# A two-layer retention/gMLP trunk on one core: gatings started one job later, loads split and moved, another square root at the end

## The chip, the core and the metric

The kernel runs on one NeuronCore of a Trainium2 chip. The metric is the device time of one execution in microseconds (us), smaller is better. Matrix products run on TensorE (PE, with its weight loads as PEld), elementwise work on VectorE (DVE) and ScalarE (ACT), and SyncE (SP) issues nearly all DMAs, in the order in which they are written. In the traces each engine takes its instructions in the order of the program, so an instruction that waits holds up all that is queued behind it on its engine.

## The reference, cut to what matters

288 tokens (256 of a prompt, 32 of a sample), model width 2048, two layers. Each layer normalises its input, multiplies it by one wide input matrix and feeds two branches; the branches are projected, gated, merged, projected again and added to the input. A final RMSNorm follows. Everything is float32.

```python
def mixer_layer(x, s0, pos, ret_chunk, norm_g, w_in, ws, ws_b, ln_g, ln_b,
                w_ret_out, w_mlp_out, w_o):
    h = rmsnorm(x, norm_g)
    z = h @ w_in
    q, k, v, gr, u, vm, gm, ar, am = jnp.split(z, _split_points(), axis=-1)
    ...
    r_branch = (jax.nn.silu(gr) * o) @ w_ret_out
    u = jax.nn.gelu(u, approximate=False)
    vn = layernorm(jax.nn.gelu(vm, approximate=False), ln_g, ln_b)
    m = spatial_gate(u, vn, ws, ws_b)
    m_branch = (jax.nn.silu(gm) * m) @ w_mlp_out
    merged = jax.nn.sigmoid(ar) * r_branch + jax.nn.sigmoid(am) * m_branch
    return x + merged @ w_o, s_new, vn
```

`spatial_gate` multiplies, in each of 8 channel groups, the layer-normed `vm` by a 128x128 position matrix `ws`, adds a bias, and multiplies by `u`. The final step is `y = x * rsqrt(mean(x^2) + eps) * final_g`.

## The kernel before

Activations lie with channels on partitions and the 288 tokens along the free dimension. A float32 product is made from three products of float32r operands: a weight tile `raw` is cast by ACT to `whi` (`to_hi`, L105), DVE subtracts to get the rest `wlo` (`to_lo`, L108), and `mm3` (L111 to L113) issues whi times the high part of the activations (`Ah`/`Bh`), whi times the low part (`Al`/`Bl`), and wlo times the high part.

The work is a list of **jobs** (L617 on): one job multiplies 256 output channels by all 2048 input channels and hands the sum in PSUM (`ps`) to an `evac_...` function. A job has four **pieces** of 4 contraction tiles each: one weight load of 512 KB, one cast, one subtraction and 24 matmuls. The main loop (from L767) writes out, for each piece, the cast of the piece four ahead, the subtraction three ahead and the load seven ahead, then the 24 matmuls, and then a `tick`: every active generator runs to its next `yield`. The evac functions and the gatings are such generators, so what they issue falls between the pieces, on each engine behind what was written before.

In each layer eight VM jobs come first. `evac_vm` transposes them through DRAM (`zd`) into a token-major tile `vmacc`, applies GELU, and the last one forms the layer norm's statistics (`state["ln"]`). Then come the jobs U0, GM0, U1, GM1 ... U7, GM7, then AM and MLP, Q/K/V/GR, AR, RET and the output projection.

A **gating** (`sgu_gen`, L281) belongs to a group g. It needs five small loads (`load_sgu`, L267: `c0`, `c1`, `wh`, `wsr`, `wsq`), zeroes a corner of the position matrix (memset, L292), scales the normed `vm` (L299, L301), splits it into `vh` (ACT) and `vl` (DVE), issues ten matmuls on TensorE (L324 to L326), and adds bias and multiplies by u (L328 to L332). It is started ahead of U job g (L631). Gating 0 issues its own loads when it starts and then waits, tick by tick, for the statistics; each gating issues the loads of the next one after its `vh`. So gating 1 starts eight pieces after gating 0, whether gating 0 is through or not.

```python
        for g in range(NPR):
            job(U0 + g, hs, evac_u, g, lambda l, g: start(sgu_gen(l, g)))
            job(GM0 + g, hs, evac_gm, g)
```

At the **start** (L711 on) SP loads the norm's gain `ng`, the first 256 channels of x (`vmacc<-in_x`), half of piece 0's weights, the next 256 channels, the other half, and then piece 1's weights, x and further pieces in turn. TensorE meanwhile runs 10 products of a zero tile (`WARM`, L717). ACT makes six zero copies (L734, L736) that are needed in the retention part alone.

At the **end** `evac_last` (L606) takes the last job in two halves, `rs_gen(last)` (L163) sums the squares over channels on TensorE, and DVE takes 1/sqrt by a bit trick and three Newton steps (`newton`, L86, 11 small instructions and a wide one that spreads the result over 128 columns, L98). TensorE turns it to the channel layout by three products with the identity (L188 to L190), and DVE scales the output (L822, L825) as it is stored.

Of the kernel before, what the change touches and what calls it, by code (L numbers as in the profile page):

```python
# [9 lines left out]
F32 = mybir.dt.float32  # L10
# [3 lines left out]
ALU = mybir.AluOpType  # L14
# [22 lines left out]
LOOK = 3  # L37
WARM = 10
RAW = 4
# [3 lines left out]
def trunk(ctx: ExitStack, tc: tile.TileContext, a, o):  # L43
# [18 lines left out]
    ident = st([P, P], "ident")  # L62
    ones = st([P, 4], "ones")
    cos = st([P, T], "cos")
    sin = st([P, T], "sin")
# [3 lines left out]
    fg = st([P, NK], "fg")  # L69
    zero = st([P, P], "wsr", bufs=2)  # L70
    qdh = [st([P, P], f"qdh{i}", F32R) for i in range(2)]
# [91 lines left out]
    def rs_gen(last=None):  # L163
# [18 lines left out]
        v = st([P, 3], "rsv")  # L182
        V.tensor_scalar(out=v, in0=p[:, 0:3], scalar1=1.0 / DM, scalar2=EPS, op0=ALU.mult, op1=ALU.add)
        yb = newton(v, 3, "rs", st([P, 3, P], "z", bufs=3))
        yield
# [4 lines left out]
        PE.matmul(p[:, 256:288], yb[:, 2], ident[:, 96:128], start=True, stop=True)  # L190
        if last is not None:
            state["rs"] = p[:, 0:T]
        else:
            rs = st([P, T], "rsb")
            S.copy(out=rs, in_=p[:, 0:T])
            S.copy(out=rst, in_=yb[:, :, 0])
            yield
            state["rs"] = rs
            cr, sr = st([P, T], "cosr"), st([P, T], "sinr")
            V.tensor_tensor(out=cr, in0=cos, in1=rs, op=ALU.mult)  # L200
            V.tensor_tensor(out=sr, in0=sin, in1=rs, op=ALU.mult)
            state["cr"], state["sr"] = cr, sr

# [77 lines left out]
    def sgu_gen(l, g):  # L281
        if g == 0:
            load_sgu(l, 0)
        lg, lb, bs, wr, wq = state.pop(("sgu", g))
# [47 lines left out]
        V.tensor_tensor(out=sg, in0=sg, in1=state.pop(("u", g)), op=ALU.mult)  # L332
        state["s", g] = sg

    def evac_u(l, g, ps):
# [236 lines left out]
    def evac_o(l, c, ps):  # L572
        x = state.pop(("x", c))
        V.tensor_tensor(out=x, in0=ps[:, :, 0:T], in1=x, op=ALU.add)
        if l + 1 < DEPTH:
            hs = state["h"]
            prep_hi(hs, c, x, ng[:, l + 1])
            sq = add_sq(c, x)
            next(sq)
            yield  # L580
            prep_lo(hs, c, x, ng[:, l + 1])
            run(sq)
            load(xs[:, 2 * c:2 * c + 2], x)
            if c == NPR - 1:
                state.pop("rs")
                start(rs_gen())
        else:
            if c == 0:
                state["yg"] = st([P, NPR, 2, T], "vmacc")
            scale_out(c, x, 0)  # L590
            scale_out(c, x, 1)
            sq = add_sq(c, x)
            next(sq)
            yield
            run(sq)
# [24 lines left out]
    for l in range(DEPTH):  # L620
# [7 lines left out]
        for c in range(NPR):  # L628
            job(VM0 + c, hs, evac_vm, c)
        for g in range(NPR):  # L630
            job(U0 + g, hs, evac_u, g, lambda l, g: start(sgu_gen(l, g)))  # L631
            job(GM0 + g, hs, evac_gm, g)
        job(AM0, hs, evac_am, 0)
# [22 lines left out]
    def emit_raw(s):  # L656
# [4 lines left out]
        r = st([P, KP, 256], "raw", bufs=RAW)  # L661
        n = KP if s else KP // 2
        for k in range(0, KP, n):
            yield
            load(r[:, k:k + n], wsrc(l, pair)[:, i * KP + k:i * KP + k + n])
        raws[s] = r
# [23 lines left out]
    def start(gen):  # L690
        active.append(gen)
# [15 lines left out]
    def prep0(c):  # L707
        prep_hi(hs0, c, x0[:, c], ng[:, 0])
        prep_lo(hs0, c, x0[:, c], ng[:, 0])

    V.memset(zero, 0.0)  # L711
    V.memset(ones, 0.0)
# [4 lines left out]
    for _ in range(WARM):  # L717
        PE.matmul(warm[:, 0:P], zero, zero, start=True, stop=True)
    load(ng, a["norm_g"])
    load0(0)  # L720
    first = emit_raw(0)
    next(first)
    next(first)
    load0(1)
    run(first)
    run(emit_raw(1))
    load0(2)
    load0(3)
    run(emit_raw(2))
    load0(4)  # L730
    load0(5)
    run(emit_raw(3))
    for q in qdh + qdl:
        S.copy(out=q, in_=zero)  # L734
    for q in w2s:
        S.copy(out=q, in_=zero)  # L736
    prep0(0)
    h0 = st([P, KP, 256], "whi", F32R, bufs=LOOK + 2)
    l0 = st([P, KP, 256], "wlo", F32R, bufs=LOOK + 1)
    r0 = raws.pop(0)  # L740
    for k in range(0, KP, KP // 2):
        ks = slice(k, k + KP // 2)
        if k:
            prep0(1)
        to_hi(r0[:, ks], h0[:, ks])
        to_lo(r0[:, ks], h0[:, ks], l0[:, ks])
    halves[0] = h0, l0
# [7 lines left out]
    prep0(5)  # L755
    run(emit_raw(4))
    load0(6)
    load0(7)
    run(emit_raw(5))
    for n, t in (("ident", ident), ("cos", cos), ("sin", sin), ("kdec", kdec), ("qdec", qdec),  # L760
                 ("final_g", fg)):
        load(t, a[n])
    emit_hi(3)
    run(emit_raw(6))

# [3 lines left out]
    for s, (j, i) in enumerate(pieces):  # L769
        l, pair, ops, fn, c, pre = jobs[j]  # L770
        emit_hi(s + LOOK + 1)
        emit_lo(s + LOOK)
        run(emit_raw(s + LOOK + RAW))
        if s == 1:
# [17 lines left out]
        def mm(k, jj):  # L792
# [4 lines left out]
                start=(kt == 0), stop=(kt == NK - 1))  # L797

        if j == last and i == NPC - 1:
            for jj in range(2):  # L800
                for k in range(KP):
                    mm(k, jj)
                last_sq = evac_last(jj, c, po[jj][:, 0:T])
        else:
            for k in range(KP):
# [8 lines left out]
        if s == 5:  # L814
            start(rs_gen())

    while active:
# [99 lines left out]
```

## Time and profile before

| | |
|---|---|
| time, median of 3 runs | 2361.43 us (2360.75 to 2362.48) |
| the profiled execution: its time / its span | 2362.0 us / 2360.2 us |
| PE busy | 2335.9 us (99% of the span) |
| PEld busy | 2333.9 us (99%) |
| DVE busy / ACT busy | 1424.1 us (60%) / 1020.2 us (43%) |
| mean DMA rate | 189 GB/s |
| granted TensorE clock, mean over the span | 0.995 of full |

The span runs from the first to the last instruction of one profiled execution; 1.8 us of that execution's time lie around it. "Busy" of PE counts overlapping, pipelined matmuls, so 99% says that it is seldom without work, and not that it runs at its peak. A row of the waits names the engine and line that waited, what it waited for, the total, the times and the longest. In a timeline, a row has start, duration, engine, line and operation, `out<-in`, and in brackets the idle time of that engine just before and what ended it.

### The profile page before, as it was taken

How to read it: one execution, taken by the hardware profiler on the slowest of the kernel's cores; microseconds unless marked ns; L12 is line 12 of the kernel's file. 1: busy time of each engine (PE TensorE's matmuls, PEld its weight loads, DVE VectorE, ACT ScalarE, POOL GpSimd, SP SyncE). 2: the span in 40 equal slices, each digit the busy share in tenths (PEclk: the TensorE clock that was granted, in tenths of full speed). 3: DMA queues.
4: the chain of work that ended last, by engine and by line, in shares of the span. 5: the costliest groups of instructions: out<-in, count | busy, mean ns of one | idle time of the engine just before them, and what ended most of it. 6: DMA issues, size and time to landing. Idle time of an engine off the chain costs nothing.

```text
span 2360.2 us, 42693 instructions
## 1 busy us (share of the span) xinstructions
PE 2335.9 (99%) x17572; PEld 2333.9 (99%) x17572; DVE 1424.1 (60%) x2145; ACT 1020.2 (43%) x1298; POOL 0.2 (0%) x4
## 2 busy tenths in 40 slices
PE   9999999999999999999999999999999999999997
PEld 9999999999999999999999999999999999999997
DVE  7567764446777774455555777544467777645554
ACT  6445543333444453334444445433344444433342
POOL 0000000000000000000000000000000000000000
PEclk9999999999999999999999999999999999999999
DMA  8855554556778785456688555445577877744553
GB/s 268 234 171 180 175 173 163 168 165 185 219 206 230 201 223 173 163 168 193 210 218 229 165 176 177 163 163 168 172 203 198 222 206 212 219 164 162 169 196 115
DMA packets 350164, 446.36 MB, mean 189 GB/s; under 512 B 193552, under 2 KB 254736, under 8 KB 349968
## 3 DMA queue, kind: packets, MB, share of 16 engines
q1 hardware_dynamic: 349968, 443.63, 62.1%
q8 instruction: 138, 2.26, 0.4%
q14 instruction: 58, 0.48, 0.1%
HBM read 412.09 MB, written 31.46 MB: 188 GB/s over the span
## 4 chain that ended last, share of the span: by engine, by line
PE 96%; DVE 2%; issue 1%; DMA 1%; SPq 0%; ACT 0%; DVEq 0%; ACTq 0%
PE ps L111 31%; PE ps L112 31%; PE ps L113 31%; PE aux L112 1%; PE aux L113 1%; PE aux L111 1%; DMA raw<-in_w_in 1%; PE aux L324 0%; DVE wlo L108 0%; DMA vmacc<-zd 0%; SPq L78 0%; PE aux L325 0%; DVE vmacc L825 0%; DVE vmacc L299 0%; PE aux L423 0%
## 5 line engine op out<-in xcount | busy, mean ns | idle before, releaser
L108 DVE TENSOR_TENSOR wlo<-raw,whi 128x1024 fp32r<-128x1024 f32 (+1 forms) x705 | 858.0, 1218 | 509.3 <-PE ps L113 321.5
L105 ACT CAST whi<-raw 128x1024 fp32r<-128x1024 f32 (+1 forms) x705 | 733.2, 1047 | 817.8 <-PE ps L112 659.1
L111 PE MATMUL ps<-Ah,whi 128*128 128x288 f32 x2816 | 832.6, 296 | 1.4 <-ACT whi L105 1.4
L113 PE MATMUL ps<-Ah,wlo 128*128 128x288 f32 x2816 | 832.0, 295 | 0.7 <-DVE wlo L108 0.7
L112 PE MATMUL ps<-Al,whi 128*128 128x288 f32 x2816 | 831.2, 295 | 0.0
L111 PE MATMUL ps<-Bh,whi 128*128 128x288 f32 x2784 | 825.2, 296 | 0.0
L112 PE MATMUL ps<-Bl,whi 128*128 128x288 f32 x2784 | 823.8, 296 | 0.0
L113 PE MATMUL ps<-Bh,wlo 128*128 128x288 f32 x2784 | 823.8, 296 | 0.0
L111 PEld LDWEIGHTS ps<-Ah,whi 128*128 128x128 f32 x2816 | 529.8, 188 | 1.9 <-ACT whi L105 1.9
L113 PEld LDWEIGHTS ps<-Ah,wlo 128*128 128x128 f32 x2816 | 529.3, 188 | 1.4 <-DVE wlo L108 1.4
L112 PEld LDWEIGHTS ps<-Al,whi 128*128 128x128 f32 x2816 | 529.1, 188 | 0.0
L112 PEld LDWEIGHTS ps<-Bl,whi 128*128 128x128 f32 x2784 | 524.4, 188 | 0.0
L111 PEld LDWEIGHTS ps<-Bh,whi 128*128 128x128 f32 x2784 | 523.9, 188 | 0.0
L113 PEld LDWEIGHTS ps<-Bh,wlo 128*128 128x128 f32 x2784 | 523.4, 188 | 0.0
L209 DVE TENSOR_TENSOR z<-ps,rsb 128x576 f32<-128x576 f32 x52 | 39.3, 755 | 61.7 <-PE ps L113 61.7
L512 ACT ACTIVATE on<-aux,gnb,gny 128x256 f32<-128x256 f32 x48 | 23.6, 562 | 65.4 <-DVE gnb L508 65.4
L216 DVE STREAM_TRANSPOSE zt<-ps 128x512 f32<-128x512 f32 x32 | 22.9, 715 | 39.8 <-PE ps L113 38.2
L503 DVE BATCH_NORM_STATS2 gst<-aux 128x6 f32<-128x256 f32 x48 | 17.5, 421 | 34.5 <-PE aux L113 34.5
L355 ACT ACTIVATE z<-z 128x576 f32<-128x576 f32 x16 | 11.0, 687 | 46.3 <-DVE z L209 46.3
L384 DVE TENSOR_TENSOR zu<-ps,cosr 128x576 f32<-128x576 f32 x16 | 12.1, 758 | 30.6 <-PE ps L113 30.6
L375 DVE TENSOR_TENSOR vmacc<-ps,z 128x576 f32<-128x576 f32 x16 | 12.1, 758 | 30.6 <-PE ps L113 30.6
L328 DVE TENSOR_TENSOR rqh<-aux,wh 128x256 f32<-128x256 f32 x32 | 13.4, 419 | 27.8 <-PE aux L325 27.8
(221 smaller groups left out, 1146.1 us busy)
## 6 DMA issues: line engine op xcount, KB each, us to landing
raw<-in_w_in SPq DMA_DIRECT2D x511, 512.0 KB, 4.7
raw<-in_w_mlp SPq DMA_DIRECT2D x64, 512.0 KB, 4.6
raw<-in_w_ret SPq DMA_DIRECT2D x64, 512.0 KB, 4.6
raw<-in_w_o SPq DMA_DIRECT2D x64, 512.0 KB, 4.6
zd<-zt SPq DMA_DIRECT2D x224, 96.0 KB, 3.7
vmacc<-zd SPq DMA_DIRECT2D x56, 384.0 KB, 5.8
c<-in_dmask SPq DMA_DIRECT2D x16, 208.0 KB, 4.8
vmacc<-in_x SPq DMA_DIRECT2D x8, 288.0 KB, 6.8
```

What stands on the lines that cost most here:

```text
L105: S.copy(out=hi, in_=src)
L108: V.tensor_tensor(out=lo, in0=src, in1=hi.bitcast(F32), op=ALU.subtract)
L111: PE.matmul(out, lh, rh, start=start, stop=False)
L112: PE.matmul(out, lh, rl, start=False, stop=False)
L113: PE.matmul(out, ll, rh, start=False, stop=stop)
L209: V.tensor_tensor(out=z, in0=ps[:, :, 0:T], in1=bc2(state["rs"]), op=ALU.mult)
L216: V.transpose(out=zt[:, :, 0:8], in_=src[:, :, 0:TP].rearrange("p j (b t) -> p j b t", t=TS))
L328: V.tensor_tensor(out=x, in0=p[:, :, 1], in1=bs[:, 0:TP].rearrange("p (b i) -> p b i", b=2), op=ALU.add)
L375: V.tensor_tensor(out=state["acc"][:, c], in0=ps[:, :, 0:T], in1=state.pop(("sig", c)), op=ALU.mult)
L384: V.tensor_tensor(out=r, in0=ps[:, :, 0:T], in1=bc2(cr), op=ALU.mult)
L503: V.bn_stats(out=bst[:, b], in_=src[b])
L512: S.activation(out=on[:, b], in_=src[b], func=AF.Identity, bias=nb[:, b:b + 1], scale=y[:, b:b + 1])
```

## The change

1. **Order of the gatings.** The jobs run U0, U1, GM0, U2, GM1 ... U7, GM6, GM7, and gating g starts ahead of U(g+1) (the last ahead of GM7). The five loads of gating 0 are issued ahead of VM job 5.
2. **The start.** `ng` and the first contraction tile of piece 0's weights are issued by ACT. SP issues x in halves first, then the second tile, the other two, then the next x and piece 1. Cast and subtraction go tile by tile, and piece 0's matmuls go by term (two of whi times high, two of whi times low, two of wlo times high per tile). The warm-up has 5 products instead of 10. The six zero copies move to after piece 24.
3. **The end.** The 1/sqrt is ACT's Sqrt, DVE's reciprocal and one Newton step. A diagonal matrix is made from it in three DVE instructions, each followed by a product with a tile of ones. That tile and a first use of Sqrt (which brings the table load) are placed at the first job of the last projection.

```diff
-WARM = 10
+WARM = 5
...
     def rs_gen(last=None):
...
+        if last is not None:
+            y, t = st([P, 3], "rsy", bufs=2), st([P, 3], "rst", bufs=2)
+            S.activation(out=t, in_=v, func=AF.Sqrt)
+            V.reciprocal(out=y, in_=t)
+            V.scalar_tensor_tensor(out=t, in0=y, scalar=-0.5, in1=y, op0=ALU.mult, op1=ALU.mult)
+            V.tensor_tensor(out=t, in0=t, in1=v, op=ALU.mult)
+            V.scalar_tensor_tensor(out=y, in0=t, scalar=1.5, in1=y, op0=ALU.add, op1=ALU.mult)
+            dg = st([P, 3, P], "z", bufs=3)
+            p = aux()
+            for b, n in ((0, P), (1, P), (2, TS)):
+                V.tensor_scalar(out=dg[:, b, 0:n], in0=ident[:, P - n:P], scalar1=y[:, b:b + 1], scalar2=None,
+                                op0=ALU.mult)
+                PE.matmul(p[:, b * P:b * P + n], state["ones"], dg[:, b, 0:n], start=True, stop=True)
+            state["rs"] = p[:, 0:T]
+            return
...
     def sgu_gen(l, g):
-        if g == 0:
-            load_sgu(l, 0)
...
+    def pre_vm(l, c):
+        if c == 5:
+            load_sgu(l, 0)
+
+    def start_sgu(l, g):
+        if g:
+            start(sgu_gen(l, g - 1))
...
+                state["ones"] = st([P, P], "so")
+                V.memset(state["ones"], 1.0)
+                S.activation(out=fgv, in_=mvl[:, :, 0], func=AF.Square)
+                S.activation(out=fgv, in_=fgv, func=AF.Sqrt)
...
-            job(VM0 + c, hs, evac_vm, c)
+            job(VM0 + c, hs, evac_vm, c, pre_vm)
         for g in range(NPR):
-            job(U0 + g, hs, evac_u, g, lambda l, g: start(sgu_gen(l, g)))
-            job(GM0 + g, hs, evac_gm, g)
+            job(U0 + g, hs, evac_u, g, start_sgu)
+            if g:
+                job(GM0 + g - 1, hs, evac_gm, g - 1)
+        job(GM0 + NPR - 1, hs, evac_gm, NPR - 1, lambda l, g: start_sgu(l, NPR))
...
+    S.dma_start(out=ng, in_=a["norm_g"])
+    load_r0(S, 0, 1)
+    load(x0[:, 0, 0], a["x"][:, 0])
+    load(x0[:, 0, 1], a["x"][:, 1])
+    load_r0(nc.sync, 1, 1)
...
-    load(ng, a["norm_g"])
-    load0(0)
...
+    load_r0(nc.sync, 2, 2)
     load0(1)
-    run(first)
-    run(emit_raw(1))
+    emit_raw(1)
...
-    for q in qdh + qdl:
-        S.copy(out=q, in_=zero)
-    for q in w2s:
-        S.copy(out=q, in_=zero)
...
+    for k in range(KP):
+        c, jj = k // 2, k % 2
+        if jj == 0:
+            hs0.alloc(c)
+        xh, xl, x, g = hs0.hi[c][:, jj], hs0.lo[c][:, jj], x0[:, c, jj], ng[:, 0, k:k + 1]
+        S.activation(out=xh, in_=x, func=AF.Copy, scale=g)
+        to_hi(r0[:, k], h0[:, k])
+        V.scalar_tensor_tensor(out=xl, in0=x, scalar=g, in1=xh.bitcast(F32), op0=ALU.mult, op1=ALU.subtract)
+        to_lo(r0[:, k], h0[:, k], l0[:, k])
...
+        def mm_by_term(k):
+            xh, xl = ops.hi[k // 2][:, k % 2], ops.lo[k // 2][:, k % 2]
+            for w, x, first in ((h, xh, k == 0), (h, xl, False), (lo, xh, False)):
+                for jj in range(2):
+                    PE.matmul(po[jj][:, 0:T], w[:, k, jj * 128:jj * 128 + 128], x, start=first, stop=False)
...
+        if s == 24:
+            for q in qdh + qdl + w2s:
+                S.copy(out=q, in_=zero)
```

**DVE around gating 0 of the first layer.** Before, from the evacuation of GM0 on (`z` from `ps`) to the end of the split that gating 0's matmuls need (`vl_1673`, `vh_1672`); `wsr_1682`, `c0_1676` and `c1_1677` belong to gating 1:

```order
L209 TENSOR_TENSOR z_1638<-ps_1485,rsb_607 128x576
L108 TENSOR_TENSOR wlo_1643<-raw_1483,whi_1601 128x1024
L292 MEMSET wsr_1682 64x64
L299 SCALAR_TENSOR_TENSOR vmacc_480<-vmacc_480,mvl_84,c0_1676 128x2x128
L301 SCALAR_TENSOR_TENSOR vmacc_480<-vmacc_480,lny_1551,c1_1677 128x2x128
L108 TENSOR_TENSOR wlo_1695<-raw_1517,whi_1641 128x1024
L108 TENSOR_TENSOR vl_1673<-vmacc_480,vh_1672 128x512
L108 TENSOR_TENSOR vh_1672<-vmacc_480,vh_1672 64x2x128
```

The change, the same stretch; the job evacuated here is U1 (`zu`), and gating 0's split is `vl_1675`, `vh_1674`:

```order
L222 TENSOR_TENSOR zu_1640<-ps_1487,rsb_603 128x576
L109 TENSOR_TENSOR wlo_1645<-raw_1485,whi_1603 128x1024
L109 TENSOR_TENSOR wlo_1690<-raw_1519,whi_1643 128x1024
L109 TENSOR_TENSOR vl_1675<-vmacc_476,vh_1674 128x512
L109 TENSOR_TENSOR vh_1674<-vmacc_476,vh_1674 64x2x128
L109 TENSOR_TENSOR wlo_1722<-raw_1570,whi_1688 128x1024
L339 TENSOR_TENSOR rqh_1750<-aux_1752,wh_937 128x256
```

Gating 1's memset and its two scalings no longer stand between gating 0's scaling and its split; they now come after gating 0 is through, with eleven instructions between its `vh_1674` and gating 1's memset. On TensorE gating 0's ten matmuls keep their place among the pieces, and gating 1's move back by three pieces.

**SP and ACT at the start.** SP before, its first six loads (`vmacc` is x, `raw_105` piece 0, `raw_109` piece 1):

```order
L78 DMA ng_75<-in_norm_g 128x32
L78 DMA vmacc_86<-in_x 128x576
L78 DMA raw_105<-in_w_in 128x512
L78 DMA vmacc_86<-in_x 128x576
L78 DMA raw_105<-in_w_in 128x512
L78 DMA raw_109<-in_w_in 128x1024
```

The change, SP's first six loads (piece 0 is `raw_88`, piece 1 `raw_107`), and ahead of them in time, on ACT, the other two:

```order
L79 DMA vmacc_87<-in_x 128x288 x2
L736 DMA raw_88<-in_w_in 128x256
L736 DMA raw_88<-in_w_in 128x512
L79 DMA vmacc_87<-in_x 128x576
L79 DMA raw_107<-in_w_in 128x1024
```

```order
L738 DMA ng_76<-in_norm_g 128x32
L736 DMA raw_88<-in_w_in 128x256
L747 ACT_TABLE_LOAD
L747 COPY fg_77<-ones_70 128x1
L767 ACTIVATE Ah0_119<-vmacc_87,ng_76 128x288
```

x is first on SP instead of second, and piece 1's weights stay SP's sixth load. On ACT two DMA issues now stand ahead of the table load.

**DVE at the end**, from the sum of squares to the first scaled output. Before:

```order
L183 TENSOR_SCALAR rsv_25506<-aux_25498 128x3
L89 TENSOR_SCALAR rst_25510<-rsv_25506 128x3
L91 TENSOR_SCALAR rsy_25509<-rst_25510 128x3
L94 SCALAR_TENSOR_TENSOR rst_25510<-rsy_25509 128x3
L95 TENSOR_TENSOR rst_25510<-rst_25510,rsv_25506 128x3
...
L98 SCALAR_TENSOR_TENSOR z_25508<-rst_25510,rsy_25509 128x384
L822 TENSOR_TENSOR vmacc_24615<-aux_25522,vmacc_24615 128x288 x2
```

The change (ACT's Sqrt of three columns lies between the first row and the second):

```order
L184 TENSOR_SCALAR rsv_25512<-aux_25504 128x3
L188 RECIPROCAL rsy_25514<-rst_25515 128x3
L189 SCALAR_TENSOR_TENSOR rst_25515<-rsy_25514 128x3
L190 TENSOR_TENSOR rst_25515<-rst_25515,rsv_25512 128x3
L191 SCALAR_TENSOR_TENSOR rsy_25514<-rst_25515,rsy_25514 128x3
L195 TENSOR_SCALAR z_25521<-ident_69,rsy_25514 128x128 x2
L195 TENSOR_SCALAR z_25521<-ident_69,rsy_25514 128x32
L858 TENSOR_TENSOR vmacc_24617<-aux_25522,vmacc_24617 128x288 x2
```

Eleven small instructions and a wide one became five small ones and three medium ones, with one small instruction on ACT. In ACT's list the Sqrt table is loaded once, at the first job of the last projection, and no table load stands behind it.

## Rows read from the trace of the kernel before

**Rows 1.** Waits of TensorE over the whole span: total us, times, longest.
```profile
PE aux L325 <- DVE vl L108: 9.0, 2, 5.6
PE aux L188 <- DVE z L98: 2.8, 1, 2.8
```
**Rows 2.** Timeline of PE, first layer: gating 0's matmuls, then gating 1's.
```profile
146.92 0.28 PE L324 MATMUL aux<-wsp,vh 128*128 128x256 f32 x1
152.77 0.47 PE L325 MATMUL aux<-wsp,vl 128*128 128x128 f32 x1 [5.57 <-DVE vl L108]
...
154.71 0.59 PE L111 MATMUL ps<-Ah,whi 128*128 128x288 f32 x1
...
157.72 0.30 PE L111 MATMUL ps<-Ah,whi 128*128 128x288 f32 x1
...
165.68 0.28 PE L324 MATMUL aux<-wsp,vh 128*128 128x256 f32 x1
...
166.74 0.38 PE L111 MATMUL ps<-Ah,whi 128*128 128x288 f32 x1
```
**Rows 3.** Busy us by stretch: sum, PE, PEld, DVE, ACT, POOL, granted clock, DMA share, GB/s.
```profile
152.00:154.00 2.00, 1.23 (x5) 1.23 (x6) 1.13 (x3) 0.00 (x0) 0.00 (x0) 0.50 0.37 119
2348.00:2350.00 2.00, 0.35 (x1) 0.35 (x2) 1.39 (x7) 0.00 (x0) 0.00 (x0) 0.76 0.00 0
```
**Rows 4.** Timeline of PE, second layer: gating 0's matmuls.
```profile
1314.96 0.28 PE L324 MATMUL aux<-wsp,vh 128*128 128x256 f32 x1
1318.67 0.47 PE L325 MATMUL aux<-wsp,vl 128*128 128x128 f32 x1 [3.42 <-DVE vl L108]
...
1320.61 0.59 PE L111 MATMUL ps<-Bh,whi 128*128 128x288 f32 x1
...
1325.07 0.30 PE L111 MATMUL ps<-Bh,whi 128*128 128x288 f32 x1
```
**Rows 5.** Timeline of DVE, first layer, where gating 0's split stands.
```profile
149.83 0.11 DVE L292 MEMSET wsr<- 64x64 f32 x1 [7.36 <-DMA wsr<-in_ws]
...
152.03 0.68 DVE L108 TENSOR_TENSOR vl<-vmacc,vh 128x512 fp32r<-128x512 f32 x1
```
**Rows 6.** Timeline of SP's queue: the load of gating 1's matrix.
```profile
144.81 0.38 SPq L78 DMA_DIRECT2D wsr<-in_ws  x1
```
**Rows 7.** Groups by line, whole span: busy us, mean ns, idle before us.
```profile
L292 DVE MEMSET wsr<- 64x64 f32 x16 | 1.8, 112 | 14.8 <-DMA wsr<-in_ws 13.9
```
**Rows 8.** Timeline of ACT: the cast ahead of gating 0's split.
```profile
142.90 0.83 ACT L105 CAST vh<-vmacc 128x768 fp32r<-128x768 f32 x1
```
**Rows 9.** Timeline of all engines at the start.
```profile
1.04 3.94 PE L718 MATMUL aux<-wsr 128*128 128x128 f32 x20 [1.04 <-DVE ones L712]
...
2.57 0.91 SPq L78 DMA_DIRECT2D raw<-in_w_in  x2
...
5.65 0.40 PE L111 MATMUL ps<-Ah,whi 128*128 128x288 f32 x1 [0.67 <-ACT whi L105]
...
9.31 1.05 ACT L105 CAST whi<-raw 128x1024 fp32r<-128x1024 f32 x1 [0.63 <-DMA raw<-in_w_in]
...
11.67 0.40 PE L113 MATMUL ps<-Ah,wlo 128*128 128x288 f32 x1 [0.35 <-DVE wlo L108]
```
**Rows 10.** Timeline of DVE at the end.
```profile
2346.86 0.16 DVE L183 TENSOR_SCALAR rsv<-aux 128x3 f32<-128x3 f32 x1 [0.92 <-PE aux L180]
...
2349.04 0.56 DVE L98 SCALAR_TENSOR_TENSOR z<-rst,rsy 128x384 f32<-128x384 f32 x1
...
2351.18 0.82 DVE L822 TENSOR_TENSOR vmacc<-aux,vmacc 128x288 f32<-128x288 f32 x2 [1.58 <-PE aux L190]
```
**Rows 11.** Groups by line: the nearest row to a three-column instruction on ACT.
```profile
L196 ACT COPY rstok<-z 128x3 f32<-128x3 f32 x2 | 0.4, 198 | 0.0
```
**Rows 12.** The chain that ended last: start, us, what.
```profile
44.66 0.22 PE aux L189 x2
...
2350.45 0.43 PE aux L189 x2
```

More of the change, by code (lines that the diff above doesn't have):

```diff
@@ L63, in trunk @@
     ones = st([P, 4], "ones")
+    fgv = st([P, 3], "fgv")
     cos = st([P, T], "cos")
@@ L69, in trunk @@
     fg = st([P, NK], "fg")
-    zero = st([P, P], "wsr", bufs=2)
+    zero = st([P, P], "so")
     qdh = [st([P, P], f"qdh{i}", F32R) for i in range(2)]
@@ L190, in rs_gen @@
         PE.matmul(p[:, 256:288], yb[:, 2], ident[:, 96:128], start=True, stop=True)
[L191 to L202, printed above, removed]
+        rs = st([P, T], "rsb")
+        S.copy(out=rs, in_=p[:, 0:T])
+        S.copy(out=rst, in_=yb[:, :, 0])
+        yield
+        state["rs"] = rs
+        cr, sr = st([P, T], "cosr"), st([P, T], "sinr")
+        V.tensor_tensor(out=cr, in0=cos, in1=rs, op=ALU.mult)
+        V.tensor_tensor(out=sr, in0=sin, in1=rs, op=ALU.mult)
+        state["cr"], state["sr"] = cr, sr
     def bc2(x):
@@ L661, in emit_raw @@
         r = st([P, KP, 256], "raw", bufs=RAW)
[L662 to L665, printed above, removed]
+        load(r, wsrc(l, pair)[:, i * KP:i * KP + KP])
         raws[s] = r
@@ L709, in prep0, with load_r0 @@
         prep_lo(hs0, c, x0[:, c], ng[:, 0])
+    r0 = st([P, KP, 256], "raw", bufs=RAW)
+    def load_r0(eng, k, n):
+        eng.dma_start(out=r0[:, k:k + n], in_=wsrc(0, VM0)[:, k:k + n])
+    S.dma_start(out=ng, in_=a["norm_g"])
[3 more added lines that the diff above has]
+    load_r0(nc.sync, 1, 1)
     V.memset(zero, 0.0)
@@ L718, in trunk @@
         PE.matmul(warm[:, 0:P], zero, zero, start=True, stop=True)
-    load(ng, a["norm_g"])
-    load0(0)
-    first = emit_raw(0)
-    next(first)
-    next(first)
+    load_r0(nc.sync, 2, 2)
     load0(1)
-    run(first)
-    run(emit_raw(1))
+    emit_raw(1)
     load0(2)
     load0(3)
-    run(emit_raw(2))
+    emit_raw(2)
     load0(4)
     load0(5)
-    run(emit_raw(3))
-    for q in qdh + qdl:
-        S.copy(out=q, in_=zero)
-    for q in w2s:
-        S.copy(out=q, in_=zero)
-    prep0(0)
+    emit_raw(3)
     h0 = st([P, KP, 256], "whi", F32R, bufs=LOOK + 2)
     l0 = st([P, KP, 256], "wlo", F32R, bufs=LOOK + 1)
[L740 to L746, printed above, removed]
+    for k in range(KP):
[7 more added lines that the diff above has]
+        to_lo(r0[:, k], h0[:, k], l0[:, k])
     halves[0] = h0, l0
@@ L755, in trunk @@
     prep0(5)
-    run(emit_raw(4))
+    emit_raw(4)
     load0(6)
     load0(7)
-    run(emit_raw(5))
+    emit_raw(5)
     for n, t in (("ident", ident), ("cos", cos), ("sin", sin), ("kdec", kdec), ("qdec", qdec),
@@ L763, in trunk @@
     emit_hi(3)
-    run(emit_raw(6))
+    emit_raw(6)
     tiles = {}
@@ L772, in trunk @@
         emit_lo(s + LOOK)
-        run(emit_raw(s + LOOK + RAW))
+        emit_raw(s + LOOK + RAW)
         if s == 1:
@@ L803, in trunk @@
                 last_sq = evac_last(jj, c, po[jj][:, 0:T])
+        elif s == 0:
+            for k in range(KP):
+                mm_by_term(k)
         else:
```

## The prediction

> **What bounds the kernel now.** I read TensorE's waits first. Nearly the whole span is matmuls one behind the other, so only a stretch in which TensorE stands still, or runs slowly, can give anything back. There are two such places that matter: 9.0 us, in two waits, in front of a gating's matmul on line 325, and 2.8 us at the end in front of line 188 [rows 1]. Everything else is the start, where the first matmuls wait for data.
>
> The timeline of PE shows what a wait on line 325 costs in all. In the first layer the gating's ten matmuls begin at 146.92, the second stands until 152.77, and the next main matmul begins at 154.71 [rows 2]. The following gating, undisturbed, takes 165.68 to 166.74, or 1.06 us, for the same ten [rows 2]. Behind the wait the main matmuls are slow too: the granted clock is 0.50 at 152 to 154 us [rows 3], the lower of the two levels (1.2 instead of 2.4 GHz), after TensorE had stood idle. Twelve main matmuls lie between 154.71 and 157.72 (0.251 each), and then 60 between 157.72 and 165.68 (0.1327 each) [rows 2]. The second layer has the same picture with a shorter wait and a longer slow stretch: 1314.96 to 1320.61 for the ten matmuls, then 18 main matmuls until 1325.07 [rows 4].
>
> Why does TensorE wait there? DVE's timeline answers: the split `vl` that the gating needs starts only at 152.03. Ahead of it stands the memset of the next gating's matrix, before which DVE was idle 7.36 us for the load of `wsr` [rows 5]. That load was issued at 144.81 [rows 6], because each gating issues the next one's loads. So gating 0 waits for data of gating 1, only because gating 1's first instructions were written ahead of gating 0's split. Over the kernel this memset waited 13.9 us for its load [rows 7], of which the first layer has half; the other gatings of a layer stand eight pieces apart and show next to nothing.
>
> **The order of the gatings.** Gating 0 started at U0 and sat through two ticks for the statistics. Started at U1 it has them, and its matmuls keep their place on TensorE. Gating 1 starts eight pieces later, and its memset stands behind gating 0's use. So the split no longer waits for the load. Is it then in time? DVE was free at 149.83 - 7.36 = 142.47 [rows 5]. Only one subtraction of a weight piece lies between; before, that and gating 1's memset and two scalings together took 149.83 to 152.03, or 2.2 us [rows 5], so it is less than that. The cast of `vh` ends at 143.73 [rows 8]. So `vl` starts by 144.7 and ends by 145.4; TensorE asks for it just behind 146.92 [rows 2]. That leaves 1.5 us or more. In the second layer the wait was shorter by 2 us, so the margin is no smaller. What comes back:
> - First layer: (154.71 - 146.92) - 1.06 = 6.73 us, and 3.01 - 12 x 0.1327 = 1.42 us from the clock; 8.15 together.
> - Second layer: (1320.61 - 1314.96) - 1.06 = 4.59 us, and 4.46 - 18 x 0.1327 = 2.07 us; 6.66 together.
> - Sum **14.8 us**. It is all on the path, since TensorE waited for nothing else there.
>
> What is late next: gating 1's load is issued where it was and lands near 149.8 [rows 5, 6]; its memset now comes two to three pieces later, near 152 us, so the wait is gone or short, and behind it stand weight pieces that TensorE needs only three pieces (about 9.6 us) on. The five early loads stand in SP's queue ahead of a weight piece and a `vmacc` read at VM job 5. Ahead of U0 the same five stood in front of the same two kinds of load, and no PE wait followed; I cost their move at nothing, hidden by weights that are issued seven pieces ahead. U and GM jobs are only exchanged, and the evacuations need their buffers no earlier.
>
> **The end.** From the first small DVE instruction at 2346.86 to the wide one at 2349.04 are eleven steps of 0.198 us; the output's scaling starts at 2351.18 [rows 10]. The change has five small DVE steps, 5 x 0.198, and Sqrt on ACT, for which the nearest row is 0.198 us [rows 11], with some 0.05 us for the hand-over. So the diagonal begins at 2346.86 + 1.24 = 2348.10, 0.94 earlier. The wide instruction took 0.56 us for 384 columns [rows 10], so I put 0.2 on each of three, and the products run beside the next one. If DVE sets the pace the last diagonal is there at 2348.7 and its short product done 0.3 later, about 2349.0, 2.15 us ahead of before. If TensorE sets it at the lower clock, the three products take as long as now, 2351.18 - 2349.60 = 1.58 us, from 2348.33: 1.27 us ahead. The products now begin inside the stretch whose mean granted clock was 0.76 [rows 3], which means that it fell near its middle, at about 2349.0; they mostly come before that. So I take **2.0 us**. Sqrt and reciprocal have no row; if each took as long as the wide instruction (0.56) 0.7 would be lost, if they took nothing 0.4 gained: ends 0.6 and 2.5 us. The table load for Sqrt and the tile of ones fall at the first job of the last projection, where ACT casts four pieces ahead: nothing.
>
> **The start.** Piece 1's weights end the last wait here: their cast starts at 9.31, when they land, and the first matmul that needs their rest starts at 11.67; from there TensorE does not stop [rows 9]. They are SP's sixth load before and after, the two loads of 2.57 taking 0.91 us to issue [rows 9], and as many bytes are ahead of them. The first matmul, at 5.65 [rows 9], will come one to two us earlier, since cast and load come tile by tile, and the six zero copies and half the warm-up no longer matter: but that is time before a wait whose end doesn't move. x moves up one slot on SP, 0.45 us, so everything may land up to that much earlier; smaller pieces may eat it. Gain 0 to 0.45 us from the loads. Against it stands the clock, the second rival below. I take **0**. The six copies at piece 24, and the matmuls by term, cost nothing: ACT is ahead by three pieces there, and the count of matmuls is the same.
>
> **Sum.** 14.8 + 2.0 + 0 = 16.8 us off the profiled execution's 2362.0: 2345.2. The median of the runs shown is 0.57 below that execution, so 2344.6 us, 0.7% faster. A measurement of this kernel can tell about 0.2%, or 4.7 us, from no change.
>
> **The rivals.**
> - *The clock is low at the start.* Of the warm-up's 20 passes each took 0.197 us [rows 9]. The same shape, a pass of line 189, took 0.11 in mid kernel and 0.215 at the end at the lower clock [rows 12]. So most of the warm-up ran at the lower clock, and half of it may not raise it; the first matmuls then come in bursts with gaps. In the two stalls the clock returned 4.95 and 6.40 us after matmuls resumed [rows 2, 4]. If that counts from when piece 0's second half is there, about 8.5, some 1 to 3 us behind 11.67 are slow and cost 0.45 of themselves, 0.5 to 1.5 us; if from 11.67, 6.4 x (1 - 0.1327/0.248) = 3.0. Price 1.5: 2346.1. The Trainium skill, TensorE: Matmul & The Clock Gate, section "What's actually happening", says that "the default state is throttled, and activity releases the throttle"; that speaks against a shorter warm-up, and by that rule this case is the likelier one. The warm-up's pace agrees with its first half. For the forecast speaks that before, full pace was reached with gaps too, around 5.65 [rows 9].
> - *One stall stays in part*, because in one layer the split still comes late, by another order of loads. It costs up to the smaller stall, 6.7 us: 2351.3. Against it is the margin above.
> - *The gating part does nothing.* The memset's wait is only what the profile names last; if the split were late for its own reasons, TensorE would wait as before, and the end alone is gained: 2359.4. Against it: DVE was idle for 7.36 us with nothing else to do.
> - *The wait moves to every later gating.* If early loads and the new order make the `wsr` loads land more than three pieces after their turn, DVE's queue, and the weight rests in it, would wait at each of the seven later gatings of a layer. One such stall costs 6.7 to 8.2 us; from the third on the gain is gone, and four make it slower: 2344.6 + 4 x 7.4 = 2374. Against it: the same seven intervals of eight pieces are there before and show hardly 0.9 us of the memset's 14.8 [rows 7].
>
> **How the numbers follow.** Forecast 0.64, low clock at the start 0.18, one stall in part 0.08, nothing from the gatings 0.05, moved waits 0.03, and 0.02 for something between. The forecast's own range is 2343.2 to 2346.0 (start -0.45 to 0, end 0.6 to 2.5). The low clock reaches to 2347.6, and half of the partly kept stall lies below 2350. So 2342.8 to 2350.0. Faster by more than 0.2% are the first three cases and most of the rest, 0.92; the fourth is "same", 0.05; the fifth is slower, 0.03.
>
> **What would show it.** Right: no PE wait on the gating's matmul behind `vl` in either layer, no stretch at clock 0.50 there, 1.06 us for gating 0's ten matmuls; the output's scaling about 4.3 us after the sum of squares' first small step became 2.3; piece 1's first rest used between 11.2 and 11.9. Wrong: a DVE wait on the memset with PE behind it, matmuls of 0.25 us past 11.7 us, or any new PE wait in VM jobs 5 to 7.

## The result, and the profile after

The changed kernel takes 2346.97 us (median of 4 runs, 2346.13 to 2347.44), the kernel before 2361.95 us on the same chip (4 runs, 2360.75 to 2362.55): a ratio of 0.9937, 95% interval 0.992 to 0.9954. It is 15.0 us faster; forecast were 16.8 us and a time of 2344.6 us, and the measured time lies inside the stated range. The profiled execution took 2346.73 us, its span 2344.9 us, 15.3 less than the span before.

TensorE's waits over the whole span, of the changed kernel, answer to [rows 1]:

```profile
engine line waited for: us in total, times, longest us
PE ps L827 <- ACT whi L106: 1.9, 2, 1.2
PE aux L197 <- DVE z L195: 1.6, 1, 1.6
...
PE ps L114 <- DVE wlo L109: 0.7, 1, 0.7
```

The 9.0 us behind the split `vl` are gone, and the 2.8 us at the end have become 1.6. The line at the top is the start (L827 are the products of piece 0).

TensorE's timeline at gating 0, in the first and in the second layer, answers to [rows 2, 4]. The rows show the first two of the ten matmuls and the main matmul behind them:

```profile
146.89 0.28 PE L335 MATMUL aux<-wsp,vh 128*128 128x256 f32 x1
147.01 0.22 PE L336 MATMUL aux<-wsp,vl 128*128 128x128 f32 x1
...
147.95 0.38 PE L112 MATMUL ps<-Ah,whi 128*128 128x288 f32 x1
...
1306.87 0.28 PE L335 MATMUL aux<-wsp,vh 128*128 128x256 f32 x1
...
1307.93 0.38 PE L112 MATMUL ps<-Bh,whi 128*128 128x288 f32 x1
```

147.95 - 146.89 = 1.06 us in both layers, with nothing between the second matmul and its neighbours. The granted clock behind it in the first layer, in windows of 2 us (the column behind the count of matmuls; from 152 to 154 it was 0.50 before [rows 3]):

```profile
150.00:152.00 2.00, 2.00 (x17) 1.00 0.81 330
152.00:154.00 2.00, 2.00 (x18) 1.00 0.75 229
154.00:156.00 2.00, 2.00 (x18) 1.00 0.67 219
```

In the second layer it is 1.00 too, in each such window from 1306 to 1316. And DVE's timeline of the first layer, against [rows 5]:

```profile
134.59 0.11 DVE L303 MEMSET wsr<- 64x64 f32 x1
...
142.93 0.69 DVE L109 TENSOR_TENSOR vl<-vmacc,vh 128x512 fp32r<-128x512 f32 x1
...
154.04 0.11 DVE L303 MEMSET wsr<- 64x64 f32 x1
```

The split starts at 142.93 instead of 152.03, and the next gating's memset stands behind it, at 154.04, without a wait.

**Where the time came from.** I follow one matmul on both timelines. The first product of the sum of squares behind the first layer's input moved from 37.02 to 36.99 us: the start gave 0.03. A product of the retention part in the first layer moved from 572.41 to 564.31, the same one in the second from 1739.74 to 1725.14: 8.1 us by the first gating, 6.5 by the second. The last sum of squares moved by the same 14.60, from 2344.66 to 2330.06. What lies behind it gave 0.7: 14.6 + 0.7 = 15.3.

The end, on DVE and PE (L195 are the three diagonals, L197 the products, L858 the output's scaling), and the granted clock there, against [rows 10]:

```profile
2332.26 0.16 DVE L184 TENSOR_SCALAR rsv<-aux 128x3 f32<-128x3 f32 x1 [0.92 <-PE aux L181]
2332.69 0.18 DVE L188 RECIPROCAL rsy<-rst 128x3 f32<-128x3 f32 x1 [0.27 <-ACT rst L187]
...
2333.49 0.63 DVE L195 TENSOR_SCALAR z<-ident,rsy 128x128 f32<-128x128 f32 x3
2335.36 0.82 DVE L858 TENSOR_TENSOR vmacc<-aux,vmacc 128x288 f32<-128x288 f32 x2 [1.23 <-PE aux L197]
```
```profile
2333.84 1.49 PE L197 MATMUL aux<-z,so 128*128 128x128 f32 x6 [1.61 <-DVE z L195]
```
```profile
2330.00:2332.00 2.00, 1.78 (x16) 1.00 0.00 0
2332.00:2334.00 2.00, 0.39 (x4) 0.62 0.00 0
2334.00:2336.00 2.00, 1.32 (x6) 0.50 0.00 0
```

From the first small step to the scaling 3.10 us instead of 4.32, that is 1.22 earlier. The products wait for nothing of DVE's after the first: they run 1.49 us at the lower clock. Behind the scaling, 2344.9 - 2335.36 = 9.54 us to the end instead of 2360.2 - 2351.18 = 9.02, so 0.52 is given back.

### The profile page after: what moved, and what is told of

Its sections match the earlier page's. It is cut to its first block, busy times and chain, and to the rows that moved or that the text cites. A ratio compares the mean times of both kernels' runs of the same rounds, so it can differ in the third digit from the quotient of the medians.

```text
span 2344.9 us, 42677 instructions
## 1 busy us (share of the span) xinstructions
PE 2329.8 (99%) x17562; PEld 2328.5 (99%) x17562; DVE 1424.4 (61%) x2144; ACT 1017.8 (43%) x1300; POOL 0.2 (0%) x4
## 4 chain that ended last, share of the span: by engine, by line
PE 99%; DVE 0%; DMA 0%; ACT 0%; SPq 0%; issue 0%; DVEq 0%
PE ps L112 32%; PE ps L114 32%; PE ps L113 32%; PE aux L113 1%; PE aux L114 1%; PE aux L112 1%; PE aux L335 0%; DMA vmacc<-in_x 0%; DVE vmacc L861 0%; PE aux L336 0%; PE aux L442 0%; PE aux L181 0%; PE aux L337 0%; PE aux L535 0%; PE aux L516 0%; ACT whi L106 0%
```

## The experiments

**My theory:** the whole of the gating gain is the wait for the next gating's load, which stood in DVE's queue ahead of the split. It goes if gating 1 starts after the split, or if its load is there in time. **The rivals:** the early loads of gating 0 do it; or the split is late for its own reasons and the later start alone gives it time.

**Later gatings and early loads, no new start or end** (`e1`).

```diff
-        if g == 0:
-            load_sgu(l, 0)
...
+    def pre_vm(l, c):
+        if c == 5:
+            load_sgu(l, 0)
+
+    def start_sgu(l, g):
+        if g:
+            start(sgu_gen(l, g - 1))
...
-            job(VM0 + c, hs, evac_vm, c)
+            job(VM0 + c, hs, evac_vm, c, pre_vm)
         for g in range(NPR):
-            job(U0 + g, hs, evac_u, g, lambda l, g: start(sgu_gen(l, g)))
-            job(GM0 + g, hs, evac_gm, g)
+            job(U0 + g, hs, evac_u, g, start_sgu)
+            if g:
+                job(GM0 + g - 1, hs, evac_gm, g - 1)
+        job(GM0 + NPR - 1, hs, evac_gm, NPR - 1, lambda l, g: start_sgu(l, NPR))
```

> The kernel before with the first part of the change alone: later gatings and the five early loads of gating 0; start and end as before. Theory (gating 0's split stood behind a memset that waited for gating 1's load; that was all of the stall): no TensorE wait on the split in either layer, 14.6 us less than before, near 2347.4 us, with the last sum of squares starting at about 2330.1 in the span as in the changed kernel. Rival (the start part matters too, since it brings other weights forward): clearly less than 14 us come back, 2350 or more.

Measured: 2347.39 us (4 runs), before 2362.48, ratio 0.9936 (0.9921 to 0.9951). Neither layer waits on the split. The time cannot be told from that of the whole change (0.9937): this part carries it.

**Its two halves apart.** Gating 0's loads ahead of VM job 5, in the old order (`e3`: of the diff above, `pre_vm` and the two removed lines alone), and the later gatings with gating 0's loads where they were (`e4`: `start_sgu` and the job order alone).

> The kernel before with gating 0's five loads ahead of VM job 5, gatings started as before. Theory: the load that is waited for is gating 1's, which is issued where it was, so the waits of 5.6 and 3.4 us stay within 1 us each: 2360 to 2363. Rival (the loads crowd SP's queue at U0, and moving them away is what helps): the waits shrink to under half, 2353 or less.

> The kernel before with the later gatings alone: each gating one job later, but gating 0 still issues its own five loads when it starts (now at U1). Theory: gating 0's own memset now waits 5 to 8 us for its load, since the statistics are already there and nothing else holds it back; the weight rests behind it on VectorE have three pieces (9.6 us) of lead, so TensorE waits 0 to 4 us per layer: 2347 to 2356. Rival (the early loads are needless): no wait, 2347.4. Rival (they are indispensable): both stalls are as large as before, 2360 or more.

The early loads alone: 2361.97 us, one time. TensorE's wait on the split stays, 8.3 us in two waits, and DVE stands as before in front of gating 1's memset:

```profile
148.90 0.11 DVE L290 MEMSET wsr<- 64x64 f32 x1 [7.69 <-DMA wsr<-in_ws]
151.10 0.68 DVE L108 TENSOR_TENSOR vl<-vmacc,vh 128x512 fp32r<-128x512 f32 x1
```

The later gatings alone: 2347.73 us, one time, and no wait on the split. I had expected DVE to wait 5 to 8 us for gating 0's own load then. It waited 0.50:

```profile
135.36 0.11 DVE L292 MEMSET wsr<- 64x64 f32 x1 [0.50 <-DMA wsr<-in_ws]
...
143.70 0.69 DVE L108 TENSOR_TENSOR vl<-vmacc,vh 128x512 fp32r<-128x512 f32 x1
```

The split is 0.8 us later than in the changed kernel (142.93), and TensorE, which uses it from 147 us on, doesn't wait. So the first rival of this run came, the early loads are needless, and the order does it all.

**The other way to take the wait away: the load, not the order.** The old order, with gating 1's five loads right behind gating 0's (`e2`), or ahead of VM job 7 and gating 0's ahead of VM job 5 (`e5`). The diff is that of `e5`; `e2` has of it the three lines on `load_sgu(l, g + 1)`, and a `load_sgu(l, 1)` behind gating 0's `load_sgu(l, 0)`.

```diff
-        if g == 0:
-            load_sgu(l, 0)
...
-        load_sgu(l, g + 1)
+        if g:
+            load_sgu(l, g + 1)
...
+    def pre_vm(l, c):
+        if c in (5, 7):
+            load_sgu(l, (c - 5) // 2)
...
-            job(VM0 + c, hs, evac_vm, c)
+            job(VM0 + c, hs, evac_vm, c, pre_vm)
```

> The kernel before in its own order of jobs and gatings; only the five loads of gating 1 are issued directly behind those of gating 0 (there are two buffers of each), and not behind gating 0's cast. The memset and the two scalings of gating 1 still stand ahead of gating 0's split on VectorE. Theory (the wait for the load is the cause, the order only its occasion): the memset no longer waits, the split is done near 145.4 us, TensorE does not wait, 13 to 15 us less: 2347 to 2349. Rival (VectorE is too full there, the order itself is the cause): the split is still late and 5 us or more of the wait stay: 2355 to 2362.

> The kernel before in its own order of jobs and gatings; gating 0's five loads are issued ahead of VM job 5 and gating 1's five ahead of VM job 7, so that not ten small loads stand in one row in SP's queue. Theory (the stall is gating 1's load, and the two-loads kernel kept part of its first-layer stall only because ten loads in a row held back a piece's weights): no TensorE wait on the split in either layer, gating 0's ten matmuls begin within 0.5 us of 146.9, 14 to 15 us less than before: 2347 to 2349. Rival (with the old order VectorE is too full in the first layer): the wait of about 1.3 us and the slow stretch behind it stay in the first layer, 2349.5 to 2352.

Measured: 2352.46 us (ratio 0.9956, 0.994 to 0.9973) and 2350.29 us (0.9947, 0.9931 to 0.9964). I had expected 2347 to 2349 of the theory in both; `e5` lies where its rival was. In neither does a memset wait for its load any more, and the second layer has no PE wait at all. The first layer keeps a piece of its stall. PE, then DVE, of the second of them:

```profile
147.13 0.39 PE L323 MATMUL aux<-wsp,vh 128*128 128x256 f32 x1 [0.19 <-ACT vh L105]
148.83 0.33 PE L324 MATMUL aux<-wsp,vl 128*128 128x128 f32 x1 [1.32 <-DVE vl L108]
...
150.50 0.59 PE L111 MATMUL ps<-Ah,whi 128*128 128x288 f32 x1
```
```profile
134.75 0.81 DVE L264 BATCH_NORM_AGGREGATE mvl<-bst 128x2 f32<-128x48 f32 x3
...
145.89 0.11 DVE L290 MEMSET wsr<- 64x64 f32 x1
...
148.09 0.69 DVE L108 TENSOR_TENSOR vl<-vmacc,vh 128x512 fp32r<-128x512 f32 x1
```

The split comes 148.09 - 134.75 = 13.34 us after the statistics, and 12.77 in the changed kernel (142.93 - 130.16); but the statistics are 4.6 us later. The extra loads go with that. In `e5` gating 1's five stand in SP's queue from 108.36 on, ahead of a weight piece that is issued at 110.79; ACT then waits 6.20 us for weights and casts them at 119.99, and the last read of `vmacc` is issued at 127.04. In `e1`, which has gating 0's early loads alone, this wait is 0.62 us, the cast starts at 114.43 and the read is issued at 122.18. With all ten in a row (`e2`), SP's queue shows the next weight piece issued at 126.54, and at 118.58 in before (1.7 us of it is that run's later start):

```profile
120.70 1.80 SPq L78 DMA_DIRECT2D c<-in_ln_b  x1
...
126.54 0.33 SPq L78 DMA_DIRECT2D raw<-in_w_in  x1
```

So both ways remove the wait for the load, which supports the theory. The second rival falls as the cause of the stall in the kernel before, where DVE stood idle for 7.36 us [rows 5], but it has a part in what is left in `e5`. There DVE works with hardly a gap from 139.18 to 148.09, and gating 1's memset and two scalings, still ahead of the split, take 145.89 to 146.96 of it. By estimate from these rows, TensorE's wait of 1.32 us would be some 0.3 without them, and would be gone if the statistics were not 4.6 us late. Moving the loads leaves some 3.8 us of the first layer's 8.1 ungained (`e5`: the next gating stands 4.50 us earlier than before, 0.20 of which is its start); the second layer gains nearly all of its own in the old order too (10.56 us at the end's first small step, so 6.1 there).

**The start and the end without the gatings** (`e6`, the changed kernel with the old order and loads) **and the end alone** (`e11`).

> The changed kernel with the order of the gatings and their loads put back as before: the start part and the end part alone. Theory: the start gives 0 (the first sum of squares on TensorE begins at 37.0 within 0.4 us, as in the kernel before), the end 0.7 to 1.2 us, both stalls stay: 2360.5 to 2362. Rival (the start part is worth something by itself): the first sum of squares begins before 36.4 and the time is under 2360.5.

> The kernel before with the new end alone. Both stalls of the gatings stay (two waits of 8 to 9.5 us in all). From the sum of squares' first small step to the output's scaling 2.5 us if the clock is still full at the three products, 3.1 if it has fallen, instead of 4.32. From the scaling to the end 9.55 if the new end is what brings the late fetch of instructions that stands 0.3 us ahead of the end in every kernel with the new end so far, 9.05 if the new start is. Span 2358.5 to 2360 in all, time 2359.5 to 2361.5: too little to be told from before by its time.

Measured: 2362.37 and 2362.04 us, one time each, not to be told from before, and a little above the ranges that I expected. Both keep the stalls (9.3 and 10.2 us in two waits, 9.0 in before). What they show lies in parts. In the start of `e6` TensorE runs piece 0 and the first matmuls of piece 1 (from 11.98 on) at the lower clock:

```profile
8.94 0.85 PE L827 MATMUL ps<-Ah,whi 128*128 128x288 f32 x2 [0.90 <-ACT whi L106]
...
11.98 0.44 PE L112 MATMUL ps<-Ah,whi 128*128 128x288 f32 x1
...
12.46 0.44 PE L114 MATMUL ps<-Ah,wlo 128*128 128x288 f32 x1
...
12.90 0.29 PE L113 MATMUL ps<-Al,whi 128*128 128x288 f32 x1
```

A pair takes 0.48 us there, 0.27 at full clock, and the first sum of squares stands at 37.88 instead of 36.99, outside the 37.0 +- 0.4 that I expected. These 0.9 us are not all the clock's. DVE has piece 1's rest ready at 10.60 + 1.22 = 11.82, 0.25 us later than in the changed kernel (10.34 + 1.23), and TensorE first uses it at 12.46 instead of 11.62. So of the 0.84 us at that point some 0.6 are the lower clock's, and the others are data that came later.

**The warm-up of 10 products put back into the changed kernel** (`e9`, `WARM = 10`).

> The changed kernel with 10 warm-up products instead of 5. If the halved warm-up is what leaves TensorE at the lower clock at the start, the first main matmuls run at 0.13 us each from about 5.2 us on, as in the profile of before; if it is chance from run to run, they may as well run at 0.24 until 8 to 10 us, as they did in the kernel with gating 0's loads alone moved, which has all 10. In either case the first sum of squares on TensorE stands at 37.0 +- 0.2, since piece 1's data, and not the pace, ends the last wait there; only a start whose low clock lasts past 11.7 us, as in the kernel with the start and the end alone, would show 37.5 or more. Time 2346 to 2347.5.

Measured: 2346.39 us, one time. The low pace is there with the full warm-up too, and ends earlier:

```profile
1.04 4.63 PE L750 MATMUL aux<-so 128*128 128x128 f32 x20 [1.04 <-DVE ones L744]
5.33 0.83 PE L827 MATMUL ps<-Ah,whi 128*128 128x288 f32 x2
...
6.92 0.48 PE L827 MATMUL ps<-Ah,whi 128*128 128x288 f32 x2
```

The kernel with gating 0's loads alone moved also has all 10, and ran its first matmuls at 0.24 us each from 5.93 to 10.43. So the length of the warm-up isn't alone in deciding this. The first sum of squares stands at 37.29, no gain, and 0.1 us outside what I expected: piece 1's weights came later, and their cast starts at 9.59, when they land.

**The start's waits taken away.** First the second load of x ahead of the last two tiles of piece 0's weights (`e8`); then, on top of it, in pieces 1 to 4 all products of `whi` ahead of those of `wlo` (`e10`).

```diff
-    load_r0(nc.sync, 2, 2)
     load0(1)
+    load_r0(nc.sync, 2, 2)
...
+        elif s < 5:
+            mm_rests_last()
```

> The changed kernel with one exchange in SP's queue at the start: the second x load ahead of the last two tiles of piece 0's weights (as the kernel before had it). Theory (the start is now held by that x load, which lands at 7.79 and behind which ACT has four instructions before piece 1's cast): x lands near 7.2 to 7.4, piece 1's first rest is used near 11.2 to 11.4, and the first sum of squares begins 0.2 to 0.5 us earlier, near 36.6. Rival (piece 1's own landing near 9.3 holds it): no change, 36.9 to 37.2.

> The changed kernel with the second load of x ahead of the two last contraction tiles of piece 0's weights, and in pieces 1 to 4 all products of whi ahead of those of wlo, so that the subtraction of a piece has 2.1 us more. If the waits for the subtraction of pieces 1 and 2 are all that is left of the start (0.56 and 0.26 us ahead of line 114, with the slow first weight loads behind them 0.8 us), TensorE runs through from the second half of piece 0 on and the first sum of squares stands at 36.0 to 36.4 instead of 36.98; the time is 2345.5 to 2346.3. If the landing of the weights takes over, at piece 2 (12.47 us) or 3, it stands at 36.7 to 37.0 and the time is the changed kernel's.

Measured: 2346.18 us, one time, and 2345.66 us (4 runs; ratio 0.9929, 0.9912 to 0.9945, which overlaps that of the changed kernel). In `e8` the rest of piece 1 is used at 11.36 instead of 11.62, and 0.2 of that is lost at piece 2, whose weights land at 12.47 in both; the first sum of squares stands at 36.98, which is the "no change" of the rival. In `e10` the waits for the rests are gone, piece 1 lands a little later, and it stands at 36.53, short of the 36.0 to 36.4 that I expected. But 8 us on, the 0.46 us are gone again: DVE waits longer for a transpose's store (1.63 us, 0.97 in the changed kernel), the first norm's 1/sqrt ends 0.8 us later, and TensorE waits for it (L204, its first product):

```profile
39.28 0.72 DVE L229 STREAM_TRANSPOSE zt<-ps 128x512 f32<-128x512 f32 x1 [1.63 <-DMA zd<-zt]
```
```profile
44.13 0.49 PE L204 MATMUL aux<-ident,z 128*128 128x128 f32 x2 [0.18 <-DVE z L99]
44.46 0.39 PE L205 MATMUL aux<-ident,z 128*128 128x128 f32 x2
```

The second product stood at 44.47 in the changed kernel, and the last sum of squares is at 2330.06 in both.

**Full-size matmuls to hold the clock at the end** (`e7`): nine of them, whose result nobody reads, behind the last sums of squares.

```diff
+            d, (w, xh) = aux(), state["busy"]
+            for _ in range(BUSY):
+                PE.matmul(d[:, 0:T], w, xh, start=True, stop=True)
```

> The changed kernel with nine extra matmuls of 288 columns into an unused PSUM tile behind the last sums of squares, so that TensorE is not idle while VectorE makes the diagonal. Theory (the products with ones ran at the lower clock, 1.49 us for the three, because TensorE had had little to do): if the extra work keeps the clock up, the three products take 0.7 to 1.0 us and the scaling starts 2.3 to 2.7 us behind the first small step, not 3.1. Rival (the clock falls from what lay before, whatever follows): still 1.4 to 1.5 us for the products and 3.1 us in all.

Measured: 2346.86 us, one time; no gain. The clock fell while they ran:

```profile
2332.05 2.30 PE L187 MATMUL aux<-Bh,whi 128*128 128x288 f32 x9
2334.14 1.32 PE L202 MATMUL aux<-z,so 128*128 128x128 f32 x6
```
```profile
2330.00:2332.00 2.00, 1.78 (x16) 1.00 0.00 0
2332.00:2334.00 2.00, 2.00 (x11) 0.58 0.00 0
2334.00:2336.00 2.00, 1.46 (x8) 0.57 0.00 0
2336.00:2338.00 2.00, 0.00 (x0) 1.00 0.50 174
```

They even hold the products up (2334.14 instead of 2333.84), so that the scaling starts at 2335.50, 3.28 us behind the first small step. This is nearer to the rival's case; what sets the moment of the fall stays open.

**The end in all thirteen profiles** (us):

| kernel | first small step to scaling | scaling to the span's end |
|---|---|---|
| before; `e1` to `e5` (old end) | 4.32; 3.91, 4.32, 4.31, 4.32, 4.31 | 9.02; 9.05, 9.04, 9.39, 9.09, 9.39 |
| changed; `e6`, `e8` to `e11` (new end) | 3.10; 2.46, 2.56, 2.46, 3.10, 2.54 | 9.54; 9.61, 9.59, 9.58, 9.54, 9.43 |
| `e7` (new end, nine matmuls) | 3.28 | 9.60 |

By the means of the first two rows the new end gains 4.25 - 2.70 = 1.55 us up to the scaling and gives back 9.55 - 9.16 = 0.39 behind it: 1.2 us net.

## Why the prediction was right or wrong

**The order of the gatings: right, in mechanism and size.** Forecast 8.15 + 6.66 = 14.8; measured 8.1 + 6.5 = 14.6. Gating 0's ten matmuls take 1.06 us as worked out, the clock stays full, and the split is earlier than the bound that I set (142.93 for "by 144.7"). The sentence that called the move of gating 0's loads free was right too, and one can go further: without it the gain is the same (`e4`).

**The end: the direction right, the size not.** The step that failed is "So I take 2.0 us". DVE's part came out as worked out: to the first diagonal 2333.49 - 2332.26 = 1.23 us (forecast 1.24), 0.63 for the three diagonals (0.6), Sqrt 0.20 and reciprocal 0.18. But the clock at the products was taken from the profile of before, where it fell near 2349.0, as though it would fall as long after the main matmuls again. They ended near 2344.7 there; in the changed kernel they ended near 2330.1 and the clock had fallen by about 2332.5, 2.4 instead of 4.4 us later, ahead of the products. So the case that the prediction priced at 1.27 us came, and was measured at 1.22. The kernels with the new end whose clock fell later (`e6`, `e8`, `e9`, `e11`) took 2.46 to 2.56, so 1.8 us less than before: near the other case, priced at 2.15. And the sum took the way from the scaling to the end as fixed; it grew by 0.52. Together 0.7 instead of 2.0, and 1.2 over all profiles.

**The start: 0 came out (0.03 us), but by another mechanism, and in part by luck.** The rest of piece 1 is first used at 11.62, 11.67 before [rows 9]. What ends this wait is another load than I thought: in the chain of waits it is the second load of x, behind which ACT casts what is left of piece 0 before piece 1 (start, duration):

```profile
2.58 5.18 DMA vmacc<-in_x
...
7.79 0.54 ACT Ah L767
...
10.34 1.24 DVE wlo L109
...
11.62 0.40 PE ps L114
```

The step that failed here is "x moves up one slot on SP, 0.45 us, so everything may land up to that much earlier". That holds for the first load of x alone (0.73, 1.16 before). The second moved back by a slot, from 2.10 to 2.58, and ACT took it up 0.58 us later (SP before, ACT before, SP in the changed kernel):

```profile
2.10 0.43 SPq L78 DMA_DIRECT2D vmacc<-in_x  x1
```
```profile
7.21 0.96 ACT L143 ACTIVATE Ah<-vmacc,ng 128x288 fp32r<-128x288 f32 x2 [1.61 <-DMA vmacc<-in_x]
```
```profile
2.58 0.43 SPq L79 DMA_DIRECT2D vmacc<-in_x  x1
```

In `e8` this load is issued at 2.11 again and ACT takes it up at 6.12; then the next data hold TensorE up, and nothing is gained. The first matmul came 0.88 us earlier (4.77), a little less than the 1 to 2 that I wrote. The low clock, my strongest rival, did come: until 8.67 the pairs on line 827 take 0.48 us. It cost nothing here, since TensorE waits for data behind it anyway; my price of 1.5 us assumed that it would last past 11.7. In `e6`, with the same start, it did, and cost some 0.6 us: that it ended in time in the changed kernel is luck. The Trainium skill, TensorE: Matmul & The Clock Gate, section "What's actually happening", calls the throttled state the default one; the warm-up's passes agree, 0.20 us each in before, 0.25 in the changed kernel and 0.23 in `e9`, against 0.11 in mid kernel [rows 12]. It is the step from there to a loss by the shorter warm-up that the runs don't bear out: with all 10 products the low pace came too.

**The other rivals** didn't come. The memset waits for no load from the second gating on, no stall is left, and the exchange of U and GM jobs cost nothing.

**The sum.** 14.6 + 0.7 = 15.3 us between the two executions, for 16.8: 0.2 of the miss is the gatings, 1.3 the end. The forecast time also subtracted the 0.57 us by which the profiled execution of before lay above its median; of the changed kernel the profiled execution lies 0.24 below its own. That makes up the rest of the 2.4 us. The measured time lies above the forecast's own 2343.2 to 2346.0; it is inside the stated range only by the room left for the low clock and for half a stall, which is not what happened, and that is luck too. The lower ends do not follow from the terms: 2344.6 - 0.45 - 0.5 is 2343.65, not 2343.2, and 2342.8 has no term at all.

What stays open is why the way from the scaling to the end is longer with the new end. The same instructions are issued at the same pace. In the changed kernel's last 2 us a fetch of instructions stands alone at about 0.3 us before the end, where it stood 1.5 us before the end in before:

```profile
GB/s 276 461 323 139 46 0 0 0 0 0 0 0 0 0 0 0 0 0 0 0 0 0 0 0 0 0 0 0 0 0 0 0 0 0 164 0 0 0 0 0
```

(40 slices of 0.05 us; the slice with 164 GB/s is the fetch, the ones at the left are the last stores.) It stands so in all kernels with the new start and the new end. In the kernel with the end alone it stands as in before, and the way is still 9.43 us. So the fetch is not the whole of it, and the two kernels with the old end that have 9.39 (`e3`, `e5`) show no such fetch in their last 2 us. I did not try to move it.

## What to carry to other kernels

When an engine takes its instructions in program order, a wait for something that is not needed yet is as bad as one for something that is. Before speeding up or moving the load, look at what stands in front of the late instruction in its queue, and move the consumer: here the order alone gave all 14.6 us, while moving the loads in the old order left some 3.8 ungained in the layer where they delayed other loads. A gain at the very start or end of a kernel should be followed to the next wait before it is counted: the 0.46 us of `e10` were gone 8 us later.

## What the runs showed of the hardware that I had not expected

- The granted clock fell at different times after the same work at the end: by the windows of 1 or 2 us about 2.4 us after the last main matmul in the changed kernel, 4.4 in before, 4.6 in `e6` and 5.5 in `e1`. Full-size matmuls that start at 2332.05 (`e7`, one run) did not keep it: it fell at about 2332.3 and came back at about 2335.7, when the products were through too. The six passes of the new end's products took 0.85 to 1.49 us.
- The first 37 us differ between kernels with the same start: the first sum of squares stands at 36.62 to 37.32 us in five of the six experiments with the start of before, and at 38.67 in `e2`, where TensorE still waited for the rests of pieces at 15 and 26 us.
- Ten small loads issued in a row held SP's queue: one of them took 1.80 us to issue, where 0.43 was usual.
